# A one-core encoder block: the two latent passes as one, cross-attention products at full width, latents made inside the query product

## The chip, the cores and the metric

One core of a Trainium2 chip runs the kernel. The metric is device time in microseconds (us) of one execution; lower is better. The core has a matrix engine (TensorE, PE in the profile; its weight loads are PEld), a vector engine (VectorE, DVE), a scalar engine (ScalarE, ACT), a general engine (GpSimd, POOL) and SyncE (SP), from whose queue most DMA transfers are issued.

## The reference

One layer of an encoder over 256 tokens of width 2048, in float32, with no masks:

```python
h = rms_norm(x, g_mix)
c_q, c_kv, k_rope, dq, dk, dv = split(h @ w_in)      # 512, 256, 64, 1024, 1024, 1024 columns
q  = rms_norm(c_q,  g_q_lat)  @ w_uq                 # 8 heads of 128 + 64 (rope)
kv = rms_norm(c_kv, g_kv_lat) @ w_ukv                # 8 heads of 128 + 128
out_mla  = softmax attention of q with (k_nope, apply_rope(k_rope)) over v
out_diff = differential attention of apply_rope(dq), apply_rope(dk), dv    # 4 heads
x = x + concat(out_mla, out_diff) @ w_out
xq, xk, xv = rms_norm(x, g_xattn) @ w_xq, rms_norm(mem, g_mem) @ w_xk, rms_norm(mem, g_mem) @ w_xv
x = x + (softmax attention of xq over xk, xv, 4 heads of 128) @ w_xo
x = x + (silu(hf @ w_gate) * (hf @ w_up)) @ w_down   # hf = rms_norm(x, g_ffn), hidden 5632
return rms_norm(x, g_final)
```

`c_q`, `c_kv` and `k_rope` are called the latents here.

## The kernel before

**Arithmetic.** Each float32 operand is split into a high part (rounded to the matrix engine's format) and a low remainder (`Split`). A product is three matmuls, high x high, high x low, low x high (`mm`, L89-93). `split_into` (L97-105) makes the parts: the cast on ACT (L99, or L102 with a scale), the remainder on DVE (L100 or L103).

**A projection** (`project`, L139-154) runs over the K tiles of 128 rows. For each piece of weights, `weights` (L113-137) issues a DMA into one of three buffers `wraw` of 2048 columns, splits it into `wh`/`wl` tiles of 1024 columns (four buffers of each), and PE does, for each K tile and each of the two token tiles (`tt`), three matmuls into an accumulator `acc` (four buffers in PSUM; four other PSUM buffers, `ps`, take transposes, scores and the rest). The left operand comes transposed: `Transposed.load` (L205-214) brings x0 (the transposed x), scaled by `g_mix` and split. The argument `before` is called ahead of each piece.

**The beginning**, in the order in which it is written. Ten dummy matmuls (L183); `gains` on SP's queue, `posi` (positions) and `invf` (frequencies) on POOL's queue (L190, L192). Then `acc_q` (L235): c_q in eight pieces of two K tiles, 512 columns, with x0 loaded between them, first two K tiles at a time, then four. POOL computes the angles of the rotations (`turns`, `prod`, L240-269), a chain of small instructions on `invf` and `posi`. Then c_kv and k_rope in a second pass over all 16 K tiles (L311), 320 columns in four pieces; the 1 MB halves of x itself (`x_res`) are loaded ahead of its first two pieces, and ACT takes their mean squares (L312-317). Then `rms_rows` (L298) normalizes c_q: DVE scales by x's norm, ACT takes the mean square, POOL the power, DVE scales again. Eight activations on ACT make sines and cosines from `turns` and `prod` (L329-332), and POOL scales those of the differential heads (L333-336). c_kv is normalized likewise (L341-343).

**The query product** of the differential heads, first half: `acc_dq = diff_project(0, 0)` (L363), 16 K tiles of 512 columns in four 1 MB pieces. Behind it are written the transposes of the latents: c_q (L364-365), and for each token tile the rotation of k_rope into `kr`, a POOL copy of it (L372), and the transposes of c_kv and kr (L366-374). The first product on them is on `cqT` (L392).

**Cross-attention.** `cross_probs` (L587-600) does half of the heads: a projection of x1 by 256 columns of `w_xq`, scaling, transposes, two score products, softmax, and the transposed probabilities `pxT`. Both halves are called (L602), then for each half a 256-column projection of mem by `w_xv`, its split (`values`, L356), and `heads_out` (L450-457), which multiplies values and probabilities into `xoT`. The output projection by `w_xo` follows (L609-610).

**What sets the order.** The program is written in one order, but a planner, which simulates the engines while the kernel is built (`schedule_with_timeline_sim`, L977), decides the order of each engine's own queue. On SP, transfers marked `keep_in_program_order` stay as written. `tc.issue_after(i)` puts what it encloses behind instruction `i` on that instruction's engine. At run time an engine takes its queue in that order.

Of the kernel before, what the change touches and what calls it, by code (L numbers as in the profile page):

```python
# [11 lines left out]
F32 = mybir.dt.float32  # L12
# [3 lines left out]
AF = mybir.ActivationFunctionType  # L16
# [3 lines left out]
P = 128  # L20
# [54 lines left out]
def encoder_block(ctx: ExitStack, tc: tile.TileContext, a, out):  # L75
# [19 lines left out]
    last_split = [None]  # L95

    def split_into(dst, src, scale=None):  # L97
        if scale is None:
            nc.scalar.copy(out=dst.h, in_=src)  # L99
            last_split[0] = nc.vector.tensor_tensor(out=dst.l, in0=src, in1=dst.h.bitcast(F32), op=ALU.subtract).ins  # L100
        else:
            nc.scalar.activation(dst.h, src, AF.Copy, scale=scale)  # L102
            nc.vector.scalar_tensor_tensor(  # L103
                out=dst.l, in0=src, scalar=scale, in1=dst.h.bitcast(F32), op0=ALU.mult, op1=ALU.subtract
            )
# [7 lines left out]
    def weights(src, fine=False, pool=None):  # L113
# [42 lines left out]
    def nat(name):  # L156
        return sb.tile([P, 512], F32, name=name, tag="nat", bufs=7)
# [41 lines left out]
    class Transposed:  # L199
# [15 lines left out]

        def __call__(self, kt):
            return self.pieces[kt // 4][:, kt % 4, :]
# [5 lines left out]
    w_in_kv = a["w_in_kv"]  # L223

    def before_cq(i):
        if i < 2:
            x0T.load(0, 2 * i, 2)
        elif i % 2 == 0:
            x0T.load(i // 2)

    def before_ckv(i):
        if i < NT:
            tc.keep_in_program_order(nc.sync.dma_start(out=x_res[i], in_=a["x"][i * P:(i + 1) * P, :]))

    acc_q = project(x0T, [a["w_in_q"][i] for i in range(8)], before=before_cq, fine=1)  # L235
# [71 lines left out]

    cqT = act_tile(name="cqT")
# [9 lines left out]

    cqs = [nat("cq") for _ in range(NT)]
    for tt in range(NT):  # L320
        rms_rows(cqs[tt], acc_q[tt], tt, QL, QL, "rq")

# [6 lines left out]
    for c_t, s_t, f0, f1 in ((cosr, sinr, 0, DR // 2), (cosd, sind, DR // 2, NF)):  # L329
        for h in range(2):  # L330
            nc.scalar.activation(s_t[:, :, h, :], turns[:, :, f0:f1], AF.Sin, scale=two_pi if h else -two_pi)
            nc.scalar.activation(c_t[:, :, h, :], prod[:, :, f0:f1], AF.Sin, scale=two_pi)
    for t in (cosd, sind):  # L333
        for tt in range(NT):
            nc.gpsimd.tensor_scalar(out=t[:, tt], in0=t[:, tt], scalar1=rstd1[:, tt:tt + 1], scalar2=None,
                                    op0=ALU.mult)
# [4 lines left out]
    ckvs = [nat("ckv") for _ in range(NT)]  # L341
    for tt in range(NT):
        rms_rows(ckvs[tt], acc[tt], tt, KVL + DR, KVL, "rkv")

    def diff_project(half, which):
        return project(x0T, [w_in[2 * which + half, i] for i in range(4)])
# [15 lines left out]

    acc_dq = diff_project(0, 0)  # L363
    for tt in range(NT):  # L364
        transposed(cqT, cqs[tt], tt, 4, g_q)
    for tt in range(NT):  # L366
        c = ckvs[tt]

        kr = nat("kr")
        nc.gpsimd.memset(kr[:, 64:192], 0.0)  # L370
        rope(kr[:, 0:64], c[:, 256:320], cosr[:, tt], sinr[:, tt], 1, 32)
        nc.gpsimd.tensor_copy(out=kr[:, 192:256], in_=kr[:, 0:64])  # L372
        transposed(ckvT, c, tt, 2, g_kv)
        transposed(krT, kr, tt, 2)

# [211 lines left out]
    def cross_probs(half):  # L587

        acc = project(x1T, [a["w_xq"][half, i] for i in range(2)])
        q = act_tile(name="xqT")  # L590
        for tt in range(NT):
            n = nat("xq")
            nc.vector.tensor_scalar(out=n[:, :256], in0=acc[tt][:, :256], scalar1=rstdx[:, tt:tt + 1], scalar2=None,
                                    op0=ALU.mult)
            transposed(q, n, tt, 2)
        t = act_tile(name="pxT")
        ps = [scores([q[:, j, :]], [xkT[:, 2 * half + j, :]]) for j in range(2)]
        for j in range(2):
            prob_T(softmax(ps[j], XD ** -0.5), t[:, 2 * j:2 * j + 2, :])
        return t  # L600
# [321 lines left out]
def _lay_out(i):  # L922
# [23 lines left out]
        "w_in_q": _pieces(w_in[:, :QL], nk=2)[0],  # L946
        "w_in_kv": _pieces(w_in[:, QL:QL + KVL + DR], 320)[0],
# [5 lines left out]
        "w_xq": _pieces(i["w_xq"][0], 256, 8),  # L953
        "w_xk": _pieces(i["w_xk"][0])[0],
        "w_xv": _pieces(i["w_xv"][0], 256, 8),
# [25 lines left out]
```

## Time and profile before

| | |
|---|---|
| median of 3 runs | 1170.62 us (1170.22 to 1171.36) |
| the profiled execution | 1172.19 us |
| its span, first to last instruction | 1170.3 us |
| PE busy | 1153.7 us, 5704 matmuls |
| DVE busy | 901.7 us |
| ACT busy | 612.2 us |
| POOL busy | 67.6 us |
| mean granted PE clock | 0.997 |
| DMA moved | 222.16 MB, mean 190 GB/s |

A row of the timeline has the start, the duration, engine, line, operation, output <- inputs with their form, how many equal ones follow each other, and in brackets how long the engine had been idle before it and what ended that. In rows `A:B` (from A to B us of the span) stand the length, then each engine's busy time with its instructions in parentheses (of PE alone, or of PE, PEld, DVE, ACT, POOL), then the granted PE clock, the busy share of the DMA engines, and GB/s. Matmuls overlap each other in the records, so a matmul's duration is longer than the distance to the next one's start; the pace is read from counts over a stretch. A row of a group ends with `| busy us, mean ns | idle time before them, and what ended it`.

### The profile page before, as it was taken

Reading aid. Unit: us, or ns where it says so; the run is one execution under the profiler, and the core shown is the slowest. Engines: PE = TensorE matmul, PEld = TensorE weight load, DVE = VectorE, ACT = ScalarE, POOL = GpSimd, SP = SyncE. Lnnn points to the kernel's source line nnn. Section 1 sums busy time; section 2 is a strip of 40 time slices with the busy share of each in tenths; the row PEclk is TensorE's granted clock in tenths of the full one; section 3 lists DMA queues with packets and bytes.
Section 4 is the critical chain, followed back from the end, with each engine's and each line's share of the span. In section 5 each row is a group of like instructions: output and inputs, shape, how many; then the busy total and the mean of one; then the engine's idle time right before and its main releaser. Section 6 shows DMA issues by size and latency. Waiting matters only on the chain.

```text
span 1170.3 us, 14804 instructions
## 1 busy us (share of the span) xinstructions
PE 1153.7 (99%) x5704; PEld 972.0 (83%) x5704; DVE 901.7 (77%) x1199; ACT 612.2 (52%) x871; POOL 67.6 (6%) x83
## 2 busy tenths in 40 slices
PE   8899999999999999999999999999999999999997
PEld 5789888888889998888888887888888888888887
DVE  6668766676768667988788787987889787797873
ACT  6736454545565555655454544554644554554552
POOL 7700000000000000000000000000000000000021
PEclk9999999999999999999999999999999999999999
DMA  8655434444755444464555555546456555555651
GB/s 284 241 169 204 150 140 164 160 158 166 291 213 179 145 149 178 178 216 177 204 190 199 171 210 216 183 170 223 180 180 216 207 188 185 211 216 194 213 205 73
DMA packets 33831, 222.16 MB, mean 190 GB/s; under 512 B 3921, under 2 KB 4305, under 8 KB 9057
## 3 DMA queue, kind: packets, MB, share of 16 engines
q1 hardware_dynamic: 32544, 217.24, 52.4%
q0 software_dynamic: 928, 3.20, 0.8%
q8 instruction: 45, 0.74, 0.3%
q10 hardware_dynamic: 288, 0.79, 0.2%
q14 instruction: 26, 0.21, 0.1%
HBM read 219.11 MB, written 2.10 MB: 189 GB/s over the span
## 4 chain that ended last, share of the span: by engine, by line
PE 94%; POOL 3%; DMA 1%; DVE 1%; issue 1%; ACT 0%; POOLq 0%; DVEq 0%; ACTq 0%
PE acc L92 27%; PE acc L93 27%; PE acc L91 27%; PE q L91 2%; PE q L92 2%; PE q L93 2%; PE pt L289 2%; POOL turns L266 1%; DMA wraw<-in_w_gu 1%; POOL prod L262 1%; POOL ang L254 1%; PE ppt L435 1%; PE psc L93 1%; PE psc L92 1%; DMA invf<-in_invf 1%
## 5 line engine op out<-in xcount | busy, mean ns | idle before, releaser
L99 ACT CAST wh<-wraw 128x1024 fp32r<-128x1024 f32 (+2 forms) x399 | 399.4, 1013 | 392.5 <-PE acc L93 356.0
L100 DVE TENSOR_TENSOR wl<-wraw,wh 128x1024 fp32r<-128x1024 f32 (+2 forms) x399 | 468.0, 1181 | 175.5 <-ACT wh L99 173.9
L92 PE MATMUL acc<-wl,x2n_h 128*128 128x512 f32 x480 | 185.5, 390 | 0.0
L93 PE MATMUL acc<-wh,x2n_l 128*128 128x512 f32 x480 | 185.3, 389 | 0.0
L91 PE MATMUL acc<-wh,x2n_h 128*128 128x512 f32 x480 | 160.5, 390 | 0.7 <-DVE res L722 0.7
L91 PEld LDWEIGHTS acc<-wh,x2n_h 128*128 128x128 f32 x480 | 90.1, 188 | 19.8 <-ACT wh L99 1.1
L93 PEld LDWEIGHTS acc<-wh,x2n_l 128*128 128x128 f32 x480 | 90.1, 188 | 19.0
L92 PEld LDWEIGHTS acc<-wl,x2n_h 128*128 128x128 f32 x480 | 90.1, 188 | 18.7
L92 PE MATMUL acc<-wl,hT_h 128*128 128x512 f32 (+1 forms) x272 | 103.7, 381 | 0.0
L93 PE MATMUL acc<-wh,hT_l 128*128 128x512 f32 (+1 forms) x272 | 103.5, 381 | 0.0
L92 PE MATMUL acc<-wl,x0T_h 128*128 128x512 f32 (+1 forms) x256 | 99.2, 388 | 3.1 <-DVE wl L100 3.1
L91 PE MATMUL acc<-wh,x0T_h 128*128 128x512 f32 (+1 forms) x256 | 95.5, 386 | 3.8 <-ACT wh L99 3.8
L93 PE MATMUL acc<-wh,x0T_l 128*128 128x512 f32 (+1 forms) x256 | 98.3, 384 | 0.0
L91 PE MATMUL acc<-wh,hT_h 128*128 128x512 f32 (+1 forms) x272 | 89.4, 382 | 0.0
L99 ACT CAST wh<-tsum 128x1024 fp32r<-128x1024 f32 x56 | 58.3, 1048 | 43.8 <-DVE tsum L690 32.4
L100 DVE TENSOR_TENSOR wl<-tsum,wh 128x1024 fp32r<-128x1024 f32 x56 | 67.9, 1218 | 8.9 <-ACT wh L99 8.8
L92 PEld LDWEIGHTS acc<-wl,x0T_h 128*128 128x128 f32 x256 | 48.4, 189 | 13.9 <-DVE wl L100 5.7
L91 PEld LDWEIGHTS acc<-wh,x0T_h 128*128 128x128 f32 x256 | 48.1, 190 | 14.2 <-ACT wh L99 5.6
L91 PEld LDWEIGHTS acc<-wh,hT_h 128*128 128x128 f32 x272 | 51.2, 188 | 10.0 <-issue 0.2
L93 PEld LDWEIGHTS acc<-wh,hT_l 128*128 128x128 f32 x272 | 51.2, 188 | 9.6
L92 PEld LDWEIGHTS acc<-wl,hT_h 128*128 128x128 f32 x272 | 51.2, 188 | 9.4
L93 PEld LDWEIGHTS acc<-wh,x0T_l 128*128 128x128 f32 x256 | 48.4, 189 | 8.3
(357 smaller groups left out, 2033.4 us busy)
## 6 DMA issues: line engine op xcount, KB each, us to landing
wraw<-in_w_gu SPq DMA_DIRECT2D x80, 1024.0 KB, 4.8
wraw<-in_w_dn SPq DMA_DIRECT2D x36, 1024.0 KB, 4.8
wraw<-in_w_in SPq DMA_DIRECT2D x24, 1024.0 KB, 4.8
wraw<-in_w_out SPq DMA_DIRECT2D x16, 1024.0 KB, 4.8
wraw<-in_w_down SPq DMA_DIRECT2D x8, 1024.0 KB, 4.8
wraw<-in_w_xk SPq DMA_DIRECT2D x4, 1024.0 KB, 5.3
wraw<-in_w_xq SPq DMA_DIRECT2D x4, 1024.0 KB, 4.8
wraw<-in_w_xv SPq DMA_DIRECT2D x4, 1024.0 KB, 4.9
```

Of the source, the lines that this page charges most:

```text
L91: nc.tensor.matmul(o, l.h, r.h, start=start, stop=False)
L92: nc.tensor.matmul(o, l.h, r.l, start=False, stop=False)
L93: nc.tensor.matmul(o, l.l, r.h, start=False, stop=stop)
L99: nc.scalar.copy(out=dst.h, in_=src)
L100: last_split[0] = nc.vector.tensor_tensor(out=dst.l, in0=src, in1=dst.h.bitcast(F32), op=ALU.subtract).ins
L254: nc.gpsimd.tensor_scalar(out=ang, in0=src, scalar1=RMAGIC, scalar2=-RMAGIC, op0=ALU.add, op1=ALU.add)
L262: nc.gpsimd.tensor_scalar(out=dst, in0=part, scalar1=c, scalar2=None, op0=ALU.mult)
L266: nc.gpsimd.tensor_tensor(out=turns, in0=turns, in1=prod, op=ALU.add)
L289: nc.tensor.transpose(out=pt[:, j * P:(j + 1) * P], in_=src[:, j * P:(j + 1) * P], identity=ident)
L435: nc.tensor.transpose(out=pt[:, kt * S + tt * P:kt * S + (tt + 1) * P], in_=p[:, tt, kt * P:(kt + 1) * P], identity=ident)
```

## The change

- **One latent pass.** c_q, c_kv and k_rope are computed together: eight pieces of two K tiles and 832 columns (`w_in_lat`). For each K tile and token tile there are three matmuls of 512 columns into `acc_q` and three of 320 columns into `acc_kv`, which now lies in the other PSUM pool. One `wh`/`wl` buffer holds one K tile.
- **x0 one K tile at a time at the start.** In the first piece the DMA of one K tile of x0 stands ahead of that of the same K tile of weights (`before_k`); K tiles 2 and 3 follow together, the others by four as before.
- **Small loads moved.** `posi` and `invf` go on SP's queue ahead of the fourth piece; the halves of x ahead of the seventh and eighth.
- **Latents inside the query product.** Normalizing, sines, rotation of k_rope and all transposes of the latents are written in a function that is called ahead of the last piece of `acc_dq`'s projection. The sine activations are put behind the last weight cast written before that (`last_cast`).
- **Cross-attention at full width.** xq is one 512-column product with all four heads' scores and softmaxes behind it; then xv is one 512-column product, and both `heads_out` follow it.

The diff, cut to its core:

```diff
@@ weights
-        step = 1024 // ncols // 2 * 2
+            if before_k is not None:
+                before_k(k)
...
+        step = max(1, 1024 // ncols // 2 * 2)
@@ the beginning
-    nc.gpsimd.dma_start(out=posi, in_=a["pos"])
-    nc.gpsimd.dma_start(out=invf, in_=a["invf"].partition_broadcast(P))
...
+        def load_one(self, k):
+            self.load(0, k, 1)
...
-    acc_q = project(x0T, [a["w_in_q"][i] for i in range(8)], before=before_cq, fine=1)
+    acc_q = [pacc.tile([P, 512], F32, name="acc", tag="acc") for _ in range(NT)]
+    acc_kv = [ps_tile("acckv") for _ in range(NT)]
+    for i in range(8):
+        if i == 1:
+            x0T.load(0, 2, 2)
+        elif i and i % 2 == 0:
+            x0T.load(i // 2)
+        if i == 3:
+            tc.keep_in_program_order(nc.sync.dma_start(out=posi, in_=a["pos"]))
+            tc.keep_in_program_order(nc.sync.dma_start(out=invf, in_=a["invf"].partition_broadcast(P)))
+        if i >= 6:
+            tc.keep_in_program_order(
+                nc.sync.dma_start(out=x_res[i - 6], in_=a["x"][(i - 6) * P:(i - 5) * P, :]))
+        for k, w in enumerate(weights(a["w_in_lat"][i], i == 0, before_k=x0T.load_one if i == 0 else None)):
+            xk = x0T(2 * i + k)
+            for tt in range(NT):
+                x = xk[:, tt * P:(tt + 1) * P]
+                mm(acc_q[tt], x, w[:, :QL], i + k == 0, i == 7 and k == 1)
+                mm(acc_kv[tt][:, :LAT], x, w[:, QL:], i + k == 0, i == 7 and k == 1)
@@ latents
-    acc = project(x0T, [w_in_kv[i] for i in range(4)], before=before_ckv)
...
+    def latents_normalized():
+        cqs = [nat("cq") for _ in range(NT)]
+        for tt in range(NT):
+            rms_rows(cqs[tt], acc_q[tt], tt, QL, QL, "rq")
+        with tc.issue_after(last_cast[0]):
...
+                    nc.scalar.activation(s_t[:, :, h, :], turns[:, :, f0:f1], AF.Sin, scale=two_pi if h else -two_pi)
+                    nc.scalar.activation(c_t[:, :, h, :], prod[:, :, f0:f1], AF.Sin, scale=two_pi)
...
+        for tt in range(NT):
+            rms_rows(ckvs[tt], acc_kv[tt], tt, KVL + DR, KVL, "rkv")
+        for tt in range(NT):
+            transposed(cqT, cqs[tt], tt, 4, g_q)
...
+    acc_dq = project(x0T, [w_in[0, i] for i in range(4)], before=lambda i: i == 3 and latents_normalized())
@@ cross-attention
-    pxT = [cross_probs(half) for half in range(2)]
+    acc = project(x1T, [a["w_xq"][i] for i in range(4)])
+    xqT = act_tile(name="xqT")
+    for tt in range(NT):
+        n = nat("xq")
+        nc.vector.tensor_scalar(out=n, in0=acc[tt], scalar1=rstdx[:, tt:tt + 1], scalar2=None, op0=ALU.mult)
+        transposed(xqT, n, tt, 4)
+
+    pxT = [act_tile(name="pxT") for _ in range(2)]
+    ps = [scores([xqT[:, h, :]], [xkT[:, h, :]]) for h in range(XH)]
+    for h in range(XH):
+        prob_T(softmax(ps[h], XD ** -0.5), pxT[h // 2][:, h % 2 * 2:h % 2 * 2 + 2, :])
+    xv = values(project(mT, [a["w_xv"][i] for i in range(4)]), rstdm)
     xoT = act_tile(name="xoT")
     for half in range(2):
-        xv = values(project(mT, [a["w_xv"][half, i] for i in range(2)]), rstdm, 256)
-        heads_out(xoT[:, 2 * half:2 * half + 2, :], [pxT[half][:, 0:2, :], pxT[half][:, 2:4, :]], xv, 0)
+        heads_out(xoT[:, 2 * half:2 * half + 2, :], [pxT[half][:, 0:2, :], pxT[half][:, 2:4, :]], xv, 2 * half)
```

More of the change, by code (lines that the diff above doesn't have):

```diff
@@ L305, in rms_rows, with diff_project @@
         nc.vector.tensor_scalar(out=c[:, :n], in0=c[:, :n], scalar1=r, scalar2=None, op0=ALU.mult)
+    def diff_project(half, which):
+        return project(x0T, [w_in[2 * which + half, i] for i in range(4)])
     cqT = act_tile(name="cqT")
@@ L339, in encoder_block @@
     soft = soft_pool.enter_context(tc.tile_pool(name="soft", bufs=2))
[L341 to L346, printed above, removed]
     def diff_rope(acc):
@@ L361, in values @@
         return t
[L363 to L374, printed above, removed]
     def stationary(wk, xT, nk, name):
```

59 lines of the change are left out of this document (21 added, 38 removed).

## Prediction

> **What bounds the kernel now.** I read the page first: which engine is busy, and whose chain ends last.
>
> ```profile
> PE 1153.7 (99%) x5704; PEld 972.0 (83%) x5704; DVE 901.7 (77%) x1199; ACT 612.2 (52%) x871; POOL 67.6 (6%) x83
> ...
> PE   8899999999999999999999999999999999999997
> ...
> PE 94%; POOL 3%; DMA 1%; DVE 1%; issue 1%; ACT 0%; POOLq 0%; DVEq 0%; ACTq 0%
> ```
>
> TensorE (PE) is the path, 94% of the chain, and by slices it is short of full only in the first two (about 58 us) and at the end. So an edit saves only what it takes off PE's stream, or off PE's waits in those first slices. The second view is a table by stretch, PE alone. The stretches are the pass for c_q, the pass for c_kv and k_rope, the differential query pass up to the first product on the latents, and three undisturbed pieces that give the pace of each width (512, 320 and 256 columns).
>
> ```profile
> 5.48:32.66 27.18, 23.60 (x98) 1.00 0.88 333
> 32.66:48.82 16.16, 14.82 (x98) 1.00 0.65 245
> 48.82:76.44 27.62, 25.63 (x114) 0.94 0.50 175
> 21.77:32.66 10.89, 10.89 (x50) 1.00 0.91 362
> 38.70:43.98 5.28, 5.28 (x38) 1.00 0.92 351
> 404.15:409.91 5.76, 5.76 (x50) 1.00 0.38 155
> ```
>
> Two of each count only reach in from the stretch before. So 512 columns pace at 10.89/48 = 0.227 us, 320 at 5.28/36 = 0.147, 256 at 5.76/48 = 0.120. The two latent passes are 96 matmuls of each kind, 96 x 0.227 + 96 x 0.147 = 35.9 us, but take 27.18 + 16.16 = 43.34: **7.5 us of waiting**. The query pass is 96 x 0.227 = 21.8, with 16 transposes of 0.11 (the 1.04 us row below, less its 0.27 tail, over seven) 1.8 more, 23.5 in all, but takes 27.62: **4.1 us lost**. The timeline, first PE, then ACT and POOL, says to what:
>
> ```profile
> 9.88 0.73 PE L91 MATMUL acc<-wh,x0T_h 128*128 128x512 f32 x2 [2.47 <-ACT wh L99]
> ...
> 48.82 1.04 PE L289 MATMUL pt<-ident,cq 128*128 128x128 f32 x8
> 50.86 0.73 PE L91 MATMUL acc<-wh,x0T_h 128*128 128x512 f32 x2 [1.00 <-ACT wh L99]
> 52.58 0.50 PE L92 MATMUL acc<-wl,x0T_h 128*128 128x512 f32 x1 [0.99 <-DVE wl L100]
> ```
>
> ```profile
> 4.82 0.60 ACT L99 CAST wh<-wraw 128x512 fp32r<-128x512 f32 x1
> 9.21 0.62 ACT L99 CAST wh<-wraw 128x512 fp32r<-128x512 f32 x1 [3.78 <-DMA wraw<-in_w_in_q]
> ...
> 41.82 0.41 ACT L331 ACTIVATE sinr<-turns 128x64 f32<-128x64 f32 x2 [1.80 <-POOL turns L255]
> ...
> 49.36 0.42 ACT L173 ACTIVATE junk<-ckv 128x256 bf16<-128x256 f32 x1 [1.40 <-DVE ckv L300]
> ```
>
> The first K tile's weights were there at 4.8; the cast of the second's, at 9.21, had waited for its DMA. At 41.82 a sine had held ACT for POOL's angles, with weight casts behind it. At 49.36 the mean square of ckv held ACT, the casts of the query pass stood behind it, and PE waited twice about a microsecond. The stretches around that show the rest, with all engines:
>
> ```profile
> 10.00:15.00 5.00, 4.12 (x15) 2.47 (x16) 4.64 (x8) 4.46 (x8) 4.57 (x6) 1.00 0.88 315
> 25.00:30.00 5.00, 5.00 (x24) 4.14 (x23) 3.25 (x4) 3.03 (x6) 4.67 (x5) 1.00 1.01 419
> ...
> 50.00:53.30 3.30, 1.46 (x5) 0.93 (x6) 3.30 (x11) 3.30 (x7) 0.88 (x2) 1.00 0.07 30
> 53.30:57.00 3.70, 3.70 (x11) 2.85 (x10) 3.70 (x7) 2.10 (x3) 1.93 (x3) 0.54 0.43 146
> ```
>
> From 50.0 to 53.3 DVE and ACT are wholly busy and PE is not. Then, for 3.7 us, the granted clock is 0.54: about (1 - 0.54) x 3.7 = 1.7 us more, which is most of what the two waits leave of the 4.1.
>
> The Trainium skill's page "TensorE: Matmul & The Clock Gate", section "Part 1: The HAM clock gate", puts the fall to half clock after at least one idle window of about 3.4 us. This trace disagrees: two waits of about 1 us brought it, and the 2.47 us wait ahead of 9.88 did not. By the page the upper ends of parts 2 and 3 below would be 1.7 us lower each; I keep what the trace shows.
>
> **Part 1: one latent pass, x0 by single K tiles.** PE's work is the same 192 matmuls, 35.9 us. What changes is how much of it stands on each K tile: 6 x (0.227 + 0.147) = 2.24 us in place of 6 x 0.227 = 1.36. The suppliers, by form:
>
> ```profile
> L99 ACT CAST wh<-wraw 128x1024 fp32r<-128x1024 f32 x12 | 12.3, 1044 | 4.8 <-DMA wraw<-in_w_in_q 3.2 <-PE acc L93 1.6
> L102 ACT ACTIVATE x0T_h<-xraw,gains 128x256 fp32r<-128x256 f32 x16 | 6.9, 499 | 2.3 <-DMA xraw<-in_xT 2.0
> L99 ACT CAST wh<-wraw 128x640 fp32r<-128x640 f32 x8 | 5.4, 717 | 0.0
> ```
>
> ```profile
> L100 DVE TENSOR_TENSOR wl<-wraw,wh 128x1024 fp32r<-128x1024 f32 x12 | 15.2, 1282 | 1.2 <-ACT wh L99 1.2
> L103 DVE SCALAR_TENSOR_TENSOR x0T_l<-xraw,gains,x0T_h 128x256 fp32r<-128x256 f32 x16 | 8.7, 600 | 3.2 <-ACT x0T_h L102 3.2
> L100 DVE TENSOR_TENSOR wl<-wraw,wh 128x640 fp32r<-128x640 f32 x8 | 7.3, 954 | 5.9 <-ACT wh L99 5.9
> ```
>
> The 832-column split doesn't occur; between 640 and 1024 I estimate 0.88 us on ACT and 1.12 on DVE. Per K tile ACT then needs 0.50 + 0.88 = 1.4 of 2.24 us and DVE 0.60 + 1.12 = 1.7 of 2.24. Before, DVE needed 0.60 + 1.28/2 = 1.2 of 1.36. So the suppliers gain room. DMA: a K tile is 131 KB of x0 and 426 KB of weights, 557 KB per 2.24 us, or 249 GB/s; the rows above moved 315 and 419. Ahead of the first product stand 595 KB (gains, x0, weights) against 562, and the first cast is 0.26 us longer, but one x0 split (0.50) fewer stands before it: I put the first matmul at 5.6 instead of 5.48. The position and frequency DMAs go from POOL's queue to SP's, behind three pieces of weights, and no longer compete with the second K tile. At about 370 GB/s (the 362 of 21.77:32.66 and up) from 4.8 us on, K tile 1 (557 KB) is there at 6.3 and PE wants it at about 7.9; K tiles 2 and 3 (1114 KB) at 9.3, the first cast by 10.2, wanted at 10.1; K tile 4 (1376 KB with its x0 piece) at 13.0, wanted at 14.6. It closes, barely at K tile 2. I leave 1.2 us of waiting; ends 0 (419 GB/s) and 4.6 (290 GB/s, below). The mean squares of x (eight on ACT) and x's two 1 MB loads move to pieces 6 and 7 of this pass; four cast K tiles ahead of PE, 9 us, cover an ACT that waits for them. Term: 0.1 + 1.2 - 7.5 = **-6.2 us**.
>
> **Part 2: latents inside the query pass.** The normalizing, sines, transposes and rope of the latents (DVE and ACT work that filled 50 to 57) are traced ahead of the last four K tiles of that pass, and the sines queue behind the casts of its first twelve. At its start PE now has casts in hand: a buffer of the latent pass falls free every 2.24 us, and one cast for two K tiles takes 1.04 us on ACT and 1.28 on DVE. So the 4.1 us should go, half-clock stretch included. What is late next is POOL:
>
> ```profile
> 8.81 1.04 POOL L244 TENSOR_SCALAR ang<-invf,posf 128x96 f32<-128x96 f32 x2 [4.48 <-DMA invf<-in_invf]
> ...
> 46.53 0.59 POOL L255 TENSOR_TENSOR prod<-prod,ang 128x192 f32<-128x192 f32 x1
> ...
> 60.26 0.37 POOL L372 COPY kr<-kr 128x64 f32<-128x64 f32 x1 [4.98 <-DVE kr L283]
> ```
>
> Its chain from the frequencies to the cosines' angles takes 47.1 - 8.8 = 38.3 us. With 3.6 MB queued ahead, the frequencies land at 13 (at 370 GB/s) to 14.5 (315) instead of 8.6, so the angles end at 51.5 to 53. The wait that this adds: the cosine on ACT for POOL; behind it on ACT stand the casts of K tiles 12 to 15, behind those DVE's remainders, and PE waits for both. The latent pass ends at 5.6 + 35.9 + 1.2 = 42.7, K tile 12 is due at 42.7 + 12 x 1.36 = 59.0, so a cast as late as 56.5 costs nothing: 3 to 5 us of cover. The second kr was ready for its transposes 13.5 us after the angles (60.6); now at 65 to 67, about where the pass ends (42.7 + 23.5 = 66.2). I leave 1.0 us; ends 0 and 4.1 (as before). Term: **-3.1 us**.
>
> **Part 3: xq and xv at 512 columns.** 384 matmuls of 256 columns become 192 of 512: 384 x 0.120 - 192 x 0.227 = 46.1 - 43.6 = 2.5 us less on PE. Casts and bytes stay. All four softmaxes now hide behind one xv pass of 21.8 us; until now they hid behind the other half. New is the end of xv: both head products need its split, and nothing else is left for PE. Before, the output product on the first half covered that:
>
> ```profile
> 420.83 0.84 ACT L102 ACTIVATE val_h<-acc,rstdm 128x256 fp32r<-128x256 f32 x2 [1.93 <-PE acc L93]
> ```
>
> The nearest price is this 0.84 for two 256-wide halves, or 0.62 for one 512-wide cast; DVE's remainder follows. PE can start on the first token tile's high part after about 0.5 us. I take 0.8; ends 0.3 and 3.2 (1.5 with the split in strict order, and 1.7 of half clock). Term: -2.5 + 0.8 = **-1.7 us**.
>
> By the same skill page, section "Back-to-back issue gap", a warm matmul costs N/2.4 ns plus 2.5 fixed; 192 fewer would then save 0.5 us, not 2.5. The paces here (0.120 and 0.227) put the fixed part at 13 ns, five times that. By the page the sum below would be 2 us smaller, 1161.6.
>
> **Sum.** -6.2 - 3.1 - 1.7 = -11.0 us. The profiled execution took 1172.19 us with a span of 1170.3; the median of the runs, 1170.62 (1170.22 to 1171.36), is near its span, so I take the sum off the median: **1159.6 us**. All terms at their good ends give -7.4 - 4.1 - 2.2, 1156.9.
>
> **The rivals.**
> - *Supply takes the place of the wait.* x0, the latent weights and x are 11 MB. At 290 GB/s, the middle of the 245 and 333 that the two passes moved until now, the last piece lands at 4.8 + 10.4/0.29 = 40.7, and its first cast (0.9) and two K tiles (4.5) end the pass at 46.1. That is 4.6 us past the bare 41.5, 3.4 more than my 1.2: 1163.0. For it: the 315 of 10:15, when DMA was 0.88 busy; against: 419 in 25:30, and that the 245 was held back by full weight buffers (DMA 0.65 busy).
> - *POOL late.* The frequencies at 16 to 18 use up the cover; PE waits 2 to 4 us around K tile 12 and a half-clock stretch adds 1.7: about 1164.5. For it: ACT already waited 1.80 for POOL; against: the 3 to 5 us of cover.
> - *The merged products save less.* If a 512-column matmul is not cheaper than two of 256, part 3 is +0.8 and the time 1162.1. For it: the paces come from different stretches. Against: the three lie on one line, 0.42 ns for each column (0.120 to 0.147 to 0.227).
> - *Slower.* The same POOL chain, with PE's order fixed: the kr transposes stand ahead of the last query matmuls, and every microsecond past about 14 of the frequencies' landing is then a microsecond of PE. It takes 11 us to undo the sum: a landing from 25 us on, for which their DMAs would have to wait behind a weight buffer. At 27 us the time is 1173. Against it: only three pieces, for which there are three buffers, stand ahead of them on SP.
>
> **How the numbers follow.** A measurement of this kernel tells about 0.2% (2.3 us) from no change. Forecast 0.57 (1156.9 to 1162); supply 0.14; POOL late 0.12; small saving 0.05; slower 0.09; several small waits that meet within 0.2% of before 0.03. Faster 0.57 + 0.14 + 0.12 + 0.05 = 0.88. The range reaches from the good ends to the POOL rival, 1156.8 to 1164.8, and leaves out the slower and same cases and the tails.
>
> **What would show it.** Right: no PE wait over 1 us before the latent pass ends, near 43; no clock under 1.00 between 45 and 70; the first product on cqT near 66 instead of 76.4; PE with 192 matmuls fewer; one PE gap under 1 us between the last xv matmul and the head products. Wrong: PE waiting for `wh` or `wl` with a DMA behind it between 20 and 40 (supply); ACT waiting for `prod` or `turns` past 56 or PE for kr (POOL); the xq and xv passes not 2.5 us shorter.

## The result, and the profile after

| | before | after |
|---|---|---|
| median of 6 runs | 1170.42 us (1168.06 to 1172.55) | 1160.22 us (1159.83 to 1161.87) |
| profiled execution, its span | 1172.19, 1170.3 us | 1160.6, 1158.8 us |

The changed kernel takes 0.9914 of the time before, 95% interval 0.9901 to 0.9927: 10.2 us less, where the prediction had 11.0 less. The page of the changed kernel, in the parts quoted of before (engines, slices, chain):

```profile
PE 1149.4 (99%) x5512; PEld 961.6 (83%) x5512; DVE 900.3 (78%) x1192; ACT 612.1 (53%) x866; POOL 69.8 (6%) x81
...
PE   9999999999999999999999999999999999999997
...
PE 98%; issue 0%; DMA 0%; DVE 0%; ACT 0%; SPq 0%; POOLq 0%; POOL 0%; DVEq 0%; ACTq 0%
```

PE does 192 matmuls fewer; its two slices at the beginning, 8 tenths busy before, are at 9 like the rest; and POOL, 3% of the chain before, is at 0%. The same table by stretch, PE alone: latent pass, query product, xq to the end of xv, the head products.

```profile
5.94:43.77 37.83, 37.76 (x192) 1.00 0.92 355
43.77:66.69 22.92, 22.92 (x109) 1.00 0.50 174
357.96:408.34 50.38, 50.22 (x250) 1.00 0.46 164
408.34:411.61 3.27, 3.22 (x24) 1.00 0.26 110
```

The one pass takes 37.83 us for 35.9 of work (before, two took 43.34). The query product takes 22.92 instead of 27.62, with no wait in it and a clock of 1.00.

The stages of the two profiles, each from the start of its first matmul, add up to where the time went; the 8 us behind the start of the last matmul are the same in all. Each kernel was also built and profiled a second time, unchanged (the runs `e10_before_again` and `e11_after_again` below), and those are in the table because they correct the first reading.

| us | before | before, again | after | after, again |
|---|---|---|---|---|
| first product at | 5.48 | 5.81 | 5.94 | 6.15 |
| latent pass | 43.34 | 41.70 | 37.83 | 38.31 |
| query product, to the first on `cqT` | 27.62 | 26.07 | 22.92 | 22.91 |
| from there to the first on x1 | 290.68 | 290.66 | 291.27 | 291.27 |
| cross-attention, to the first on x2 | 79.36 | 79.36 | 77.82 | 77.82 |
| feed-forward, to the last matmul | 715.91 | 716.21 | 715.06 | 714.97 |
| span | 1170.3 | 1167.8 | 1158.8 | 1159.4 |

By the means of the two: start and pass -4.1, query product and what follows it -3.3, cross-attention -1.5, feed-forward -1.0; together -10.0, near the 10.2 of the medians. The first pair of profiles alone would give -11.5.

Two ways to state a wait occur below. The bracket of a PE row is the idle time by the records, in which matmuls overlap. A wait "beyond the pace" is the distance between the starts of two matmuls less the pace of the first (0.227 us at 512 columns, 0.147 at 320, 0.11 for a transpose); at full clock it is 0.15 to 0.4 us longer, and it is what the stages of the table lose.

### The profile page after: what moved, and what is told of

Same layout as the page of the kernel before. It is cut to its first block, busy times and chain, and to the rows that moved or that the text cites. A ratio compares the mean times of both kernels' runs of the same rounds, so it can differ in the third digit from the quotient of the medians.

```text
span 1158.8 us, 14403 instructions
## 1 busy us (share of the span) xinstructions
PE 1149.4 (99%) x5512; PEld 961.6 (83%) x5512; DVE 900.3 (78%) x1192; ACT 612.1 (53%) x866; POOL 69.8 (6%) x81
## 4 chain that ended last, share of the span: by engine, by line
PE 98%; issue 0%; DMA 0%; DVE 0%; ACT 0%; SPq 0%; POOLq 0%; POOL 0%; DVEq 0%; ACTq 0%
PE acc L91 28%; PE acc L92 28%; PE acc L93 28%; PE q L91 2%; PE q L92 2%; PE q L93 2%; PE pt L301 2%; PE ppt L448 1%; PE psc L93 1%; PE psc L92 1%; PE psc L91 1%; PE acckv L91 0%; PE acckv L93 0%; PE acckv L92 0%; PE pt L824 0%
## 5 line engine op out<-in xcount | busy, mean ns | idle before, releaser
L92 PE MATMUL acc<-wl,x0T_h 128*128 128x512 f32 x224 | 88.2, 394 | 0.1
L93 PE MATMUL acc<-wh,x0T_l 128*128 128x512 f32 x224 | 87.9, 393 | 0.0
L91 PE MATMUL acc<-wh,x0T_h 128*128 128x512 f32 x224 | 87.7, 396 | 0.0
L91 PEld LDWEIGHTS acc<-wh,x0T_h 128*128 128x128 f32 x224 | 42.3, 189 | 9.0 <-ACT wh L99 1.1
L92 PEld LDWEIGHTS acc<-wl,x0T_h 128*128 128x128 f32 x224 | 42.2, 188 | 8.3 <-DVE wl L100 0.8
L93 PEld LDWEIGHTS acc<-wh,x0T_l 128*128 128x128 f32 x224 | 42.2, 188 | 7.4
```

Source lines behind the costliest of these rows:

```text
L91: nc.tensor.matmul(o, l.h, r.h, start=start, stop=False)
L92: nc.tensor.matmul(o, l.h, r.l, start=False, stop=False)
L93: nc.tensor.matmul(o, l.l, r.h, start=False, stop=stop)
```

## The experiments

Every ratio is to the kernel before, run on the same chip.

**Two profiles again**, of unchanged kernels. They were taken to see whether the 0.85 us by which the feed-forward stage, untouched by the change, got shorter belongs to one execution.

> The kernel before, unchanged, built and profiled once more, for its feed-forward stage (from x2T's first product to the last matmul: 715.91 us in the first profile, with one PE wait of 0.67 us at 729 for a weight transfer that took 6.85 us). Theory (that late transfer belongs to the one execution): no such wait at 729, and 714.9 to 715.3 us, or a wait at another place. Rival (it belongs to the kernel): the same wait at 729 and 715.7 to 716.1 us.

> The changed kernel, unchanged, built and profiled once more. Theory (start and feed-forward stage vary with each execution): the first weights land between 4.9 and 5.7 and the first product starts between 5.9 and 6.7, the latent pass takes 37 to 38.5 us, and the feed-forward stage 714.9 to 716.0 us, with a wait of under 1 us somewhere in it or none. Rival (both are fixed by the kernel): first product at 5.94, latent pass 37.83, feed-forward stage 715.06, each within 0.05 us.

Measured: before took 1169.53 us, after 1161.2. In the second profile of before PE waited ahead of 984 (0.93 us in the bracket, 1.09 beyond the pace), not at 729; in that of after nowhere in this stage. The theory of the first run had allowed for another place, but its cause, the accident of one execution, does not fit: the place moved, the loss stayed (716.21). In after the start varied as the theory said (5.94, 6.15); this stage hardly did (715.06, 714.97). The fourteen profiles of this study sort cleanly. The seven with cross-attention in halves (before twice, `e3`, `e4`, `e6`, `e9`, `e12`) took 715.50 to 716.87 us in the feed-forward stage, mean 716.12, and each has such a wait (0.21 to 0.93 us in the bracket); the seven with whole cross-attention took 714.93 to 715.06, mean 714.97, and none has. So 1.15 us there come with part 3: `e3` is the changed kernel with nothing but the halves put back. The wait of `e12_pass_and_place`, as DVE and PE show it, and the DMA in a window of 0.6 us, in which the late transfer was issued (a queue's row has its packets, MB and share; a row of issues the count, KB and us to landing):

```profile
719.53 1.22 DVE L699 TENSOR_TENSOR tsum<-wraw 128x1024 f32<-128x1024 f32 x1 [2.02 <-DMA wraw<-in_w_gu]
720.67 1.28 DVE L736 TENSOR_TENSOR res<-acc,res 128x512 f32<-128x512 f32 x2
```

```profile
721.50 0.47 PE L91 MATMUL acc<-wh,x2n_h 128*128 128x512 f32 x1 [0.90 <-DVE res L736]
```

```profile
q8 instruction: 1, 0.02, 10.0%
issues: line engine op xcount, KB each, median us to landing
wraw<-in_w_gu SPq DMA_DIRECT2D x1, 1024.0 KB, 7.4
```

A weight transfer that takes 4.8 us in the median of the page took 7.4. DVE stood 2.02 us for it, so its work on `res`, for which PE waits, came late. Just behind the issue a packet of the instruction queue (q8) was on one of the DMA engines. In all seven the transfers that came late and held PE were issued 273.4 or 531.2 to 532.1 us after the stage's first product; in before and `e12`, a q8 packet comes at 274 and at 532 to 533. In six of the seven only one of the two places had a wait. In after, with 192 matmuls fewer ahead of it, the nearest packets come at 260 and 518, and the transfer issued beside the first of them is not late (after, 695.7 to 696.3):

```profile
q8 instruction: 1, 0.02, 9.7%
issues: line engine op xcount, KB each, median us to landing
wraw<-in_w_gu SPq DMA_DIRECT2D x1, 1024.0 KB, 4.8
```

That the shorter program moves the instruction loads away from two tight transfers is argued from this, not shown: here too a packet and a transfer meet, without harm, and other transfers of after take up to 7.0 us where nothing waits for them.

**The four corners of parts 1 and 2.** Three kernels equal before with an addition: the place of the latents alone, the one pass alone, and both; x0 by pairs, the small loads on POOL's queue and the halves of cross-attention stay.

```diff
# e4_before_latents_inside: before, and
+    acc = project(x0T, [w_in_kv[i] for i in range(4)], before=before_ckv,
+                  accs=[ps_tile("acckv") for _ in range(NT)])
...
+    acc_dq = project(x0T, [w_in[0, i] for i in range(4)], before=lambda i: i == 3 and latents_normalized())
# e9_one_pass_only: before, and the one loop over K with acc_q and acc_kv,
# the latents in their old place
# e12_pass_and_place: before, with both
```

> The kernel before with only one part of the change: the latents written inside the query product, with the sines behind its first casts; two latent passes stay (the 320-column one accumulates in the other PSUM pool so that its sums can live longer). Theory (the place of the latents is what counts): the query product up to the first product on cqT, 27.6 us, becomes 23 to 24, and the 1.2 us wait behind the sine in the second pass goes too; total 1164.8 to 1166. Rival (the gain needs the one pass's casts in hand): it stays over 26, total over 1168.

> The kernel before with only the latent pass in one: x0 in pairs, position and frequency loads on POOL's queue, latents normalized ahead of the query product and transposed behind it, cross attention in halves. Theory (the one pass by itself removes the latent pass's waits, and the latents' place costs what it cost in the run that put the latents back, 3.5 us): latent pass ends at 43.2 to 44.5, query product with what follows 317 to 318 us up to x1T's first product, total 1164 to 1167 us. Rival (those 3.5 us came from the angles, which ended at 53.7 there, because the two small loads stood behind weights; with these loads early the angles end near 47 and the latents are in time): query product with what follows 314.5 to 316 us, total 1162 to 1164 us. If the pass itself still waited as before, it would end at 46 or later and the total would be 1167 us or more.

> The kernel before with two parts of the change: the latent pass in one, and the latents made inside the query product. x0 in pairs, the small loads on POOL's queue and cross attention in halves stay as before. Alone, the place of the latents gave 0.9973 of the time before, the one pass 0.9994, because a sine then still held the casts of the pass (pass 40.43 us long). Theory (the pass only gains when the sines are out of its way, so the two together give more than their sum): latent pass 37.5 to 38.8 us, query product 22.9, what follows up to x1T 291.3, cross 79.36, total 1161.5 to 1164 us, ratio 0.993 to 0.9955. Rival (the two simply add up): ratio 0.9967, 1166 to 1167 us, with a latent pass of 39.5 to 41 us.

| | time, us | ratio (95%) | pass | query product | to x1 |
|---|---|---|---|---|---|
| place alone | 1167.12 | 0.9973 (0.9961 to 0.9984) | 42.71 | 22.90 | 291.28 |
| one pass alone | 1169.76 | 0.9994 (0.9984 to 1.0005) | 40.43 | 23.82 | 294.42 |
| both | 1163.58 | 0.9944 (0.9924 to 0.9963) | 38.98 | 22.91 | 291.28 |

The place alone gave somewhat less than expected (1164.8 to 1166). The wait behind the sine is gone, but two of 0.86 and 0.39 us beyond the pace stand in the second pass (ahead of 33.9 and 37.9). Its query product has no wait, with the old passes before it. **One pass alone gains nothing that can be measured**, against my theory of 1164 to 1167 and its rival; what came is the third case of the expectation, a pass that still waits and ends past 46 (46.76). The pass got shorter by only 1 to 3 us, and the latents came late at the other end. The first is a sine on ACT (ACT, then PE, of `e9_one_pass_only`):

```profile
40.60 0.40 ACT L345 ACTIVATE sinr<-turns 128x64 f32<-128x64 f32 x2 [2.54 <-POOL turns L268]
40.91 1.66 ACT L99 CAST wh<-wraw 128x832 fp32r<-128x832 f32 x2
```

```profile
41.83 0.50 PE L91 MATMUL acc<-wh,x0T_h 128*128 128x512 f32 x1 [1.16 <-ACT wh L99]
...
70.58 0.50 PE L91 MATMUL acc<-wh,cqT_h 128*128 128x512 f32 x1 [0.78 <-ACT cqT_h L99]
...
73.00 0.79 PE L93 MATMUL acc<-wh,cqT_l 128*128 128x512 f32 x1 [1.09 <-DVE cqT_l L100]
```

The sine stands on ACT ahead of the last casts of the pass, and waits for POOL as it did in before (1.80 there). With both parts the sines stand behind the casts, and ACT in `e12_pass_and_place` takes them without a wait:

```profile
51.92 1.28 ACT L347 ACT_TABLE_LOAD   x1
53.21 0.26 ACT L347 ACTIVATE sinr<-turns 128x64 f32<-128x64 f32 x1
```

Adding up would give 0.9967. The interval of `e12` ends at 0.9963, but the two single ratios have intervals of their own, so the times alone leave this open; the stages do not. From one pass alone to both, the pass loses 1.45 us, about the wait at 41.83 (1.33 beyond the pace), though at 38.98 it is a little over the 37.5 to 38.8 expected. The place is worth 3.3 us from the end of the pass to x1 with the old passes (314.18, against 317.5 in the mean of before's two profiles) and 4.1 with the one pass (314.19, against 318.24).

**The latents back in their place**, in the changed kernel.

```diff
-    acc_dq = project(x0T, [w_in[0, i] for i in range(4)], before=lambda i: i == 3 and latents_normalized())
+    # rms_rows, sines, ckvs written here, as before
+    acc_dq = project(x0T, [w_in[0, i] for i in range(4)])
+    # transposes and rope written here
```

> The changed kernel with the latents put back where they were: normalized and sines ahead of the query product, transposes and rope written behind it, no order on the sines. Theory (their place is what made DVE and ACT late for the query product): from the end of the latent pass to the first product on cqT 22.9 us becomes 26 to 28, with PE waits of 1 us and more for wh or wl and a stretch at half clock; total 1163.5 to 1165. Rival (the one pass, with casts in hand at its end, did it; the place of the latents hardly matters): at most 1 us more, total under 1161.5.

Measured 1163.74 us, ratio 0.9947 (0.9932 to 0.9962): 0.33 points of the 0.86 gained are lost. The query product took 24.78 (not the 26 to 28 expected) and what follows 292.91, together 3.5 us more than after. The latent pass itself took 37.30: the angles come later here than in `e9`, and the planner put the sines behind its casts, so the pass has no wait for them although the latents stand in their old place. The waits beyond the pace are 0.82 us at 57 and 0.94 and 1.26 at the first products on `cqT`, with no half clock. The total is as the theory said, the waits are at the other end of the product.

**Small loads.** First put back on POOL's queue in the changed kernel, then moved to SP's in the kernel before, then moved later in the changed kernel.

```diff
# e1_small_loads_back: after, and
+    nc.gpsimd.dma_start(out=posi, in_=a["pos"])
+    nc.gpsimd.dma_start(out=invf, in_=a["invf"].partition_broadcast(P))
# e6_before_small_loads: before, and ahead of the fourth piece
+            tc.keep_in_program_order(nc.sync.dma_start(out=posi, in_=a["pos"]))
+            tc.keep_in_program_order(nc.sync.dma_start(out=invf, in_=a["invf"].partition_broadcast(P)))
# e7_late_angles: after, and
-        if i == 3:
+        if i == 6:
```

> The changed kernel with one part undone: positions and frequencies are issued from POOL's queue at the very start again. Theory (the small transfers hold up the first weights): the weights of the first K tiles land 1 to 2 us later (the second ones, at 8.1 in the changed kernel, at 9 to 10), PE waits 1 to 2 us more in the latent pass, which ends at 44.8 to 45.8 instead of 43.77; total 1161 to 1162. Rival (a K tile of 2.24 us of matmuls covers the delay, the place of these loads is worth nothing): the pass ends within 0.4 us of 43.77. Either way POOL's chain starts some 6 us sooner and nothing after 44 changes by more than 0.5 us.

> The kernel before with one thing changed: positions and frequencies on SP's queue ahead of the fourth piece of weights; two latent passes. Theory (the small transfers cost the first weights 1 to 2 us, and a K tile of 1.36 us of matmuls cannot cover that): the second K tile's weights land at 7 to 8 instead of 9.2, the 2.6 us wait at 7 shrinks to 0.5 to 1.5; but POOL's angles come 5 us later and the planner puts sines and mean squares elsewhere, so that the query product keeps waits of 4 us or more; total 1169 to 1172. Rival (the waits at the start are set by the bytes and PE's work for each K tile, not by the small transfers): the wait at 7 stays over 2 us.

> The changed kernel with positions and frequencies moved further back on SP's queue, from ahead of the fourth piece to ahead of the seventh: they land at 23 to 25 instead of 15.1, POOL's angles end at 62 to 63 instead of 53.7. Theory (what the slower rival priced: once the angles' delay exceeds the cover, PE waits in its fixed order for what needs them): the kr transposes, which stand ahead of the product on cqT in this build's PE order, hold PE 4 to 9 us near 67, with a half-clock stretch behind it; total 1165 to 1171. Rival (the planner sees the delay and puts other work there): total under 1162.5.

`e1` took 1161.72 us, 0.9928 (0.9913 to 0.9943), with a pass of 38.33 that ended at 44.48. The total is where the theory had it, but the two profiles of after end their pass at 43.77 and 44.46, and the two intervals overlap: with x0 by single K tiles, a worth of the move is not shown, and one of up to 1.5 us not excluded. `e6` took **1178.13 us, 1.0066 (1.0047 to 1.0084): slower**. The second K tile's weights came at 6.34 instead of 9.19, and the wait for them is gone, as the theory said (one of 1.35 us comes at the third K tile). But the frequencies landed at 12.5 instead of 8.6, and the planner wrote another order for PE: the transposes of ckv and kr, which in before stood inside the query product or at its end (first row, before), now all stand ahead of it (the other rows, `e6`; then its stretches with all engines):

```profile
76.30 0.38 PE L289 MATMUL pt<-ident,kr 128*128 128x128 f32 x2
...
52.56 0.69 PE L290 MATMUL pt<-ident,ckv 128*128 128x128 f32 x2 [4.00 <-DVE ckv L306]
54.02 0.45 PE L290 MATMUL pt<-ident,kr 128*128 128x128 f32 x1 [0.77 <-DVE kr L284]
...
57.29 0.80 PE L91 MATMUL acc<-wh,x0T_h 128*128 128x512 f32 x1 [1.42 <-ACT wh L99]
```

```profile
50.00:55.00 5.00, 1.67 (x6) 0.98 (x6) 3.81 (x18) 1.73 (x7) 4.64 (x10) 0.66 0.00 0
55.00:60.00 5.00, 3.55 (x9) 2.03 (x9) 4.49 (x8) 4.75 (x7) 0.35 (x1) 0.50 0.01 3
```

These three waits are 7 us beyond the pace (4.17, 1.08 and 1.78), and the clock is 0.66 and 0.50 around them. The time is above what was expected: later angles had been counted, but not an order that puts PE behind them. `e7` took 1164.07 us, 0.9948 (0.9931 to 0.9965). Its frequencies landed at 26.20, 11 us later than in after; the angles ended near 65.5 (ACT), and PE waited for kr (PE):

```profile
61.99 0.41 ACT L346 ACTIVATE sinr<-turns 128x64 f32<-128x64 f32 x2 [4.12 <-POOL turns L267]
65.53 0.41 ACT L347 ACTIVATE cosr<-prod 128x64 f32<-128x64 f32 x2 [2.73 <-POOL prod L267]
```

```profile
67.85 0.30 PE L301 MATMUL pt<-ident,kr 128*128 128x128 f32 x1 [0.37 <-DVE kr L295]
68.76 0.33 PE L301 MATMUL pt<-ident,kr 128*128 128x128 f32 x1 [0.39 <-POOL kr L363]
69.59 0.54 PE L301 MATMUL pt<-ident,kr 128*128 128x128 f32 x2 [0.51 <-DVE kr L295]
```

Waits of 2.3 us beyond the pace, 1.7 of half clock behind them (0.63 from 70.5 to 74), together 4.2 in the table's terms, and a total just under the 1165 to 1171 expected. The planner had put the last casts of the query product ahead of the sines, and the second kr was copied 4 us after the angles; in the changed kernel it is copied 14 us after them.

**x0 by pairs again, cross-attention in halves again, a start and a tail of my own.**

```diff
# e5_x0_pairs: after, and
-        if i == 1:
-            x0T.load(0, 2, 2)
-        elif i and i % 2 == 0:
+        if i < 2:
+            x0T.load(0, 2 * i, 2)
+        elif i % 2 == 0:
# e3_cross_halves: after, with cross_probs(half) and the loop over xv halves of before
# e8_start_and_tail: after, with the first K tile's weights loaded and cast in columns
# 0-512 and 512-832, and xv's last piece token tile by token tile
+            for c0, c1 in ((0, 512), (512, ncols)) if fine and k == 0 else ((0, ncols),):
...
+    xv = values(project(mT, [a["w_xv"][i] for i in range(4)], tail_by_token=True), rstdm)
```

> The changed kernel with x0's first two K tiles loaded in one transfer again, ahead of the first weights. Theory (only the bytes ahead count, 131 KB at about 300 GB/s, and one x0 split more ahead of the first cast): the first matmul starts 0.4 to 0.6 us later than it otherwise would (5.9 to 6.2 in the runs with single K tiles whose first weights landed by 5.3), the second K tile as soon as before; the latent pass ends within 0.5 us of 43.5 to 43.8; total 1160 to 1161. Rival (the single K tiles are what removed the wait for the second weights): the pass ends 1.5 us or more later.

> The changed kernel with cross-attention in halves of 256 columns, as before. Theory (per-matmul cost of 13 ns, 192 matmuls more, less a gap of 0.7 us at the end of xv): from the first xq matmul to the first gate matmul 77.82 us becomes 79.2 to 79.6; total 1161.5 to 1162.3, which the times can hardly tell, the stretch can. Rival (the fixed cost is 2.5 ns): the stretch becomes 77.5 to 77.8, no difference or a shade faster.

> The changed kernel with two additions. The first K tile's weights come and are cast in two column parts, 512 and 320, so that c_q's matmuls can start on the first; theory: first matmul 0.5 to 0.8 us sooner (5.2 to 5.7), but the second K tile's weights still land at about 8, so the latent pass ends at most 0.4 us sooner. And the last four K tiles of xv run token tile by token tile, so that the first one's split is done when the second ends; theory: the 0.3 us gap at the end of xv and the 0.2 us one in the head products go, cross-attention 77.8 becomes 77.1 to 77.5. Total 1159.3 to 1160.2. Rival (the wait only moves to the second token tile's split): cross-attention stays at 77.7 or more.

| | time, us | ratio (95%) | first product | pass | cross | feed-forward |
|---|---|---|---|---|---|---|
| x0 by pairs | 1159.93 | 0.9914 (0.9900 to 0.9929) | 6.54 | 36.62 | 77.82 | 714.97 |
| cross in halves | 1164.16 | 0.9950 (0.9935 to 0.9964) | 6.62 | 38.07 | 79.36 | 716.00 |
| start and tail | 1160.64 | 0.9919 (0.9904 to 0.9934) | 5.19 | 38.67 | 77.86 | 714.95 |

With the small loads moved, single K tiles are worth nothing: by pairs PE begins 0.6 us later, and the pass ends at 43.17 instead of 43.77, within what the theory had. But each of these two edits was undone only with the other in place. `e12` has neither (its halves of cross-attention come 310 us later), and its second K tile's weights came 2.5 us later than in `e5` (ACT, `e12`, then `e5`):

```profile
9.49 0.88 ACT L99 CAST wh<-wraw 128x832 fp32r<-128x832 f32 x1 [3.34 <-DMA wraw<-in_w_in_lat]
...
7.00 0.89 ACT L99 CAST wh<-wraw 128x832 fp32r<-128x832 f32 x1 [0.51 <-DMA wraw<-in_w_in_lat]
```

With x0 by pairs these weights landed at 8.19 to 9.47 us in the five profiles with the small loads on POOL's queue, and at 6.34 and 6.98 in the two with them on SP's. The waits of the one pass, beyond its 35.9 us, are 3.1 with neither edit (`e12`), 2.4 with single K tiles alone (`e1`), 0.7 with the small loads alone (`e5`), 1.9 and 2.4 with both. Each is one execution, so the size is open, but that these edits are worth nothing together is not shown.

An earlier start is worth nothing: `e8` began 0.75 us sooner and ended its pass at 43.87, since it waited for the second K tile instead. The tail by token tiles only moved its gaps (77.86, where 77.1 to 77.5 was expected). No version beat the changed kernel by more than the noise. Halves in cross-attention cost 1.54 us in that stage, as the theory said, 1.0 in the feed-forward stage, and 0.9 at the start, where the first weights had landed at 5.66, for the same code as 4.98 in after; so the total is 2 us above the 1161.5 to 1162.3 expected.

## Why the prediction was right, and where it was not

**Right**: faster, 0.6 us from the forecast. PE was the path, and the gain is waits and 192 matmuls taken off it. That the sum is so near is in part luck: by the means, parts 1 to 3 gave 8.9 of the 11.0 us, and 1.0 came from a stage that the prediction did not have.

**Part 1, -6.2 us: -5.05 in the first pair of profiles, -4.1 by the means.** Two things in it failed. First a size, the supply at the start. I let the second K tile's 557 KB come by themselves at 370 GB/s, there at 6.3. They were there at 8.09 (ACT), and not because the DMA moved so little (PE alone, from the first weights' landing to the second's):

```profile
5.00 0.89 ACT L99 CAST wh<-wraw 128x832 fp32r<-128x832 f32 x1 [1.07 <-DMA wraw<-in_w_in_lat]
...
8.11 0.89 ACT L99 CAST wh<-wraw 128x832 fp32r<-128x832 f32 x1 [1.81 <-DMA wraw<-in_w_in_lat]
```

```profile
4.98:8.09 3.11, 3.06 (x11) 1.00 0.89 321
```

At 321 GB/s it moved 3.11 x 321 = 998 KB in that time, for 557 KB that were wanted next; transfers further back in the queue had been issued by then, and took the rest. In the second profile the second K tile's weights came at 7.06, but those of the third and fourth at 11.38 (10.70 in the first), where I had 9.3. The first product came at 5.94, not 5.6. Waits were 1.97 (2.4 in the second profile, one of 1.26 beyond the pace at the third K tile), not 1.2; 1.7 of them lie before 16.6 us, and 0.8 of those are the first four matmuls, which take from 5.94 to 7.48 instead of 0.75 us. From 10 to 30 us the DMA brought 370 to 427 GB/s and from 15 us on PE waited for no cast of the pass: the supply rival fell.

Second, the cause of the "7.5 gone". I gave it to the one pass. `e9` shows that the pass alone leaves 4.5 us of waits. What freed the casts at its end was that the sines no longer stood ahead of them in ACT's queue: by the place of the latents in `e12`, by later angles in `e2`. I had quoted that wait (1.80 for `turns`) and put it in the wrong part. The sum hid it, since both parts came together. The rest of the waits are nearly all at the start; how much of them the order of the first transfers takes away is open (`e12`, `e1` and `e5` above). The 7.5 was also one execution's: the second profile of before has 41.70 - 35.9 = 5.8.

**Part 2, -3.1 us: -4.1 in the first pair, -3.3 by the means.** No wait is left where I kept 1.0. The frequencies landed at 15.07 (forecast 13 to 14.5), and POOL's chain of 38.5 us ended at 53.7 (51.5 to 53):

```profile
53.75 0.26 ACT L347 ACTIVATE cosr<-prod 128x64 f32<-128x64 f32 x1 [1.69 <-POOL prod L267]
...
55.01 1.98 ACT L99 CAST wh<-wraw 128x1024 fp32r<-128x1024 f32 x2
```

The casts behind it began at 55.0, within the 56.5 that I had worked out. The second kr was there at 67.67, past my 65 to 67; it did no harm, for the transposes of kr stand behind the first products on `cqT` (from 69.19 on). Six transposes that before had ahead of `cqT` now stand there; at 0.11 each they make the 0.6 us by which the following stretch got longer. The rival of a late POOL fell at this landing. My reason, that PE has casts of the one pass in hand, was not needed: in `e4` the query product has no wait either, with the old passes before it.

**Part 3, -1.7 us: -1.54, and 1.15 more in the feed-forward stage.** The gaps at the end of xv, beyond the pace, are 0.32 and 0.20 and two of 0.1, against 0.8 forecast (PE):

```profile
407.79 0.39 PE L93 MATMUL acc<-wh,mT_l 128*128 128x512 f32 x1
408.34 0.39 PE L91 MATMUL po<-pxT_h,val_h 128*128 128x256 f32 x1 [0.16 <-ACT val_h L102]
...
408.80 0.28 PE L92 MATMUL po<-pxT_l,val_h 128*128 128x256 f32 x1
409.12 0.38 PE L93 MATMUL po<-pxT_h,val_l 128*128 128x256 f32 x1
```

So what is left for the matmuls is 1.54 + 0.73 = 2.27, against 2.5 forecast. The rival of no saving fell, and `e3` gave the 1.54 back. By the 2.5 ns fixed part in the Trainium skill's page "TensorE: Matmul & The Clock Gate", section "Back-to-back issue gap", this stage would, by an estimate, have been 0.2 us longer (0.5 saved, 0.73 lost); the trace does not agree. That section of the Trainium skill gives the formula for an isolated matmul and says that in a stream weight loads and matmuls together set the spacing, so the prediction compared the stream with a case it is not. The feed-forward gain was not in the prediction at all.

**The slower rival** was real, and mispriced. In the kernel before, the move of the small loads costs 8 us (`e6`), with PE's order rewritten. It is not part 2 alone that removes this: `e2` has the move and not part 2, and its query product and what follows take 317.69 us, against 318.24 in `e9`, which has the small loads early. Both keep the transposes of ckv and kr behind the query product. What makes the planner choose `e6`'s order stays open. In the changed kernel a landing at 26.2 us cost 4 us, not the 12 that I gave it ("every microsecond past about 14"): the forecast held the order fixed, and the planner wrote another one for late angles.

**The half clock**, 1.7 us of part 2's gain, does not come with every execution. The second profile of before has the same two waits (1.01 and 0.98 in the brackets) and this clock (PE alone):

```profile
48.69:51.99 3.30, 1.45 (x5) 1.00 0.07 30
51.99:55.69 3.70, 3.70 (x20) 1.00 0.43 146
```

The first had 0.54 there after the same 1.46 of 3.30 us busy. Likewise with the waits of 0.94 and 1.26 beyond the pace that `e9` (first fence) and `e2` share:

```profile
69.50:73.50 4.00, 2.13 (x8) 0.92 0.13 18
73.50:77.20 3.70, 3.70 (x13) 0.62 0.69 266
```

```profile
67.24:71.24 4.00, 2.14 (x9) 1.00 0.15 17
71.24:74.94 3.70, 3.70 (x19) 1.00 0.67 270
```

So my sentence that the two waits "brought it" was too strong. The Trainium skill, in "Part 1: The HAM clock gate" of the same page, says that the window in which activity is counted runs freely and doesn't begin with the work. These pairs agree with that: equal waits, one time caught and one time not. They disagree with its condition of a whole idle window of about 3.4 us, for PE was busy 1.46 of 3.30.

The traces show more. Every stretch of constant clock between the first change and the last is a multiple of 3.41 us (in before 47.79, 3.41 and 1109.33), so the changes lie on a grid. On it both waits of before fall into one step of 3.41 us (49.86 to 53.27, PE busy 1.43 of 3.41), and so do those of `e9` but for the last 0.1 us (69.46 to 72.87, 1.68 busy). The second profile of before has a border at 50.94, inside its second wait, and `e2` at 68.93, between the two. That fits a phase of the grid that decides which waits are caught. It is not shown as a rule: a step with 1.75 us busy (second profile of before) was not followed by half clock, one with 2.16 (`e7`) was.

The times scatter with it. The ten runs of `e9` sort by the mean granted clock: four at 0.998 or more took 1167.15 to 1168.48 us, six at 0.997 or less 1169.46 to 1171.03. Of the four of `e7` two took 1162.6 and 1162.7 (0.999), two 1165.4 and 1165.8 (0.997; the profiled one is of these).

## What to carry to other kernels

Before a wait is put down to the edit that lies next to it, look at what stands ahead of the waiting cast in its engine's queue; here the one pass gained only when a sine no longer stood ahead of its last casts. Where two edits may cover for each other, undo both as well as each: undone singly, the single K tiles of x0 and the place of the small loads both seemed worth nothing. Profile both kernels twice before the terms of a sum are taken from waits: before's own stages moved by 1.6 us from one execution to the next, as much as one of the terms. A transfer moved to make room can change the order in which everything behind its data is written: the same move brought early weights sooner and cost 8 us in one kernel, and cost nothing that could be measured in the others.

## What had not been expected of the hardware

- While several transfers are issued, the next in the queue does not get all that the DMA moves: 557 KB took 3.1 us in one profile, in which 998 KB moved (321 GB/s), and 1.9 us in the other (353 GB/s moved).
- With the same code the first weights landed at 4.98 us in one profile and 5.66 in another; the first product came at 5.94 to 6.62.
- Equal waits brought a granted clock of 0.54 in one execution and 1.00 in another; its changes lie on a grid of 3.41 us.
- One or two weight transfers took 6.7 to 7.4 us instead of 4.8 and held PE in the feed-forward stage, in every profile of a kernel with cross-attention in halves, at one or both of two places in it.
